# Sliding-window attention in a two-layer trunk: masked differences of values, one PSUM bank for both kv heads, scalar columns, queries by SyncE

## The chip, the cores and the metric

One Trainium2 chip, one core. The metric is the device time of one execution in microseconds. The kernel before takes 1153.45 us (median of 3 runs, 1150.15 to 1155.98).

## The reference, cut to what matters

A decoder trunk of two layers over 1024 tokens of 1024 features, in float32. Layer 0 is a pooling and short-convolution mixer with two large projections. Layer 1, which the change touches, is attention over a window of 128 tokens with 16 query heads of 64 columns, 2 key/value heads (8 query heads each) and a learned sink per head:

```
proj = y @ w_in + b_in                      # q, k, v and the gate z
q, k = partial_rotary(q), partial_rotary(k)
scores = (q . k) / 8, masked to 0 <= i + 128 - j < 128 over the previous and the own block
m   = max(max_j scores, sink)
p   = exp(scores - m);  p = p / (sum p + exp(sink - m))
out = p @ [v of the previous block; v of the own block]
h   = h + (out * silu(z)) @ w_out + b_out
return rms_norm(h, g)
```

Blocks are of 128 queries. A query i sees the keys j > i of the previous block and the keys j <= i of its own, so each pair of positions (i, j) in a 128x128 tile is taken from exactly one of the two blocks.

## The kernel before, in words

All products run on TensorE in float32r with operands split into a high and a low part (`split`: ScalarE casts the high part, VectorE subtracts for the low one), so a product is three matmuls. Layer 0's and layer 1's input projections use Strassen's scheme over pairs of output tiles (`Strassen.pair`; layer 1 has nine pairs, and their first partial products lie in `c1_dram` and are loaded back into `t3` tiles). `t3` is a pool of 128x512 tiles, 14 of them in layer 1. `W` is a pool of 9 raw tiles (weights, residual rows `h2`), `U` one of 16 split weight tiles that first hold the operands of Strassen's sums and later the output projection's weights.

The order of TensorE is the order of the program. The other engines' orders are a planner's, made from the program order and the planner's own costs; a tile whose buffers are all taken waits for a release.

Layer 1: the pairs for k and v, then four for q (stored transposed as high and low parts in `q_dram`), then four for the gate z (`z_pair`, L1122; silu on ScalarE in `gates`, stored in `z_dram`). Block 0 of the attention and the scores of block 1 are put between the products of the gate's pairs (`steps`). After them the loop over b from 1 to 8 (L1256) does, for each half js of the heads (two groups g of four heads each; one "step" below):

- `queries` (L1057): the queries of block b+1, loaded by GpSimd's queue straight into `qT` tiles, one step ahead;
- `probs` (L1143): the eight tiles of probabilities of block b are transposed on TensorE into a bank per group, split, and each part is masked twice by GpSimd (`affine_select`): strictly lower for the previous block's values, upper for the own;
- `scores` (L1065) of block b+1 in four pairs of heads: per head two matmuls against the keys of two blocks, then VectorE lays one block over the other by `copy_predicated` (so one 128x128 tile holds each score once), takes the maximum of a row, joins it with the sink (L1089), and ScalarE takes the exponential with its sum; `norm` scales by the reciprocal on GpSimd;
- `project` (L1192): the output projection of block b-1, eight groups of three matmuls; the pairs of scores come in at groups 1, 3, 4 and 6;
- `attend` (L1165): eight matmuls of 512 columns for the values of block b. The stationary operand holds a head's high and low values side by side, so a bank gets both in different partitions: ScalarE copies one half, VectorE adds it to the other, multiplies by the gate tile (loaded here by SyncE), and the result is split into `aH`, `aL`.

`summed` and `finish` add the residual, square, and apply the root (`rsqrt_mean` with n = 1, L130) and the final weights per block. PSUM has eight banks: during layer 1's pairs four called `b` and four `psB`; before the loop this pool is released and one with two `psA`, two `psD` and four `psB` made. The last four of the split weights needed first (`WO_FIRST`) are fetched among the gate's steps and split after the gates (L1254).

Of the kernel before, what the change touches and what calls it, by code (L numbers as in the profile page):

```python
# [18 lines left out]
P = 128  # L19
# [15 lines left out]
QT_BUFS = 6  # L35
# [39 lines left out]
def trunk(ctx, tc, x, xT, g1, pos, cols, w_in, w_pool, w_out, w_l1, b_kv, sinks, w_o, g_fin, out):  # L75
# [20 lines left out]
    def psA(name=None):  # L96
        if "l1" in pools:
            return psB()
        turn[0] += 1
        return pools["ps"].tile([P, HALF], F32, name=name or ("psA", "psD")[turn[0] % 2], bufs=2)  # L100
# [29 lines left out]
    def rsqrt_mean(pool, out_ap, sums, n, part=None):  # L130
# [13 lines left out]
        for it in range(3):  # L144
            if n == 1:
# [4 lines left out]
            stt(out=out_ap if it == 2 else y, in0=a, scalar=1.5, in1=y, op0=ALU.add, op1=ALU.mult)  # L150
# [714 lines left out]
    pools["ps"] = ps = tc.alloc_tile_pool(name="ps1", bufs=4, space=PSUM, reuse_waits="tile")  # L865
    pools["l1"] = True
# [37 lines left out]
    pools["t3n"] = 14  # L904
# [141 lines left out]
    qTs = {}  # L1046

    def load_q(b, js):
        if (b, js) not in qTs and b < NB:
            qTs[b, js] = [pe.tile([P, HALF], F32R, name="qT", bufs=QT_BUFS) for _ in range(2)]  # L1050
            for g, t in enumerate(qTs[b, js]):
                h = 8 * g + 4 * js
                nc.gpsimd.dma_start(out=t.rearrange("p (h c) -> p h c", c=P), in_=q_dram[
                    :, :, h:h + 4, b * P:(b + 1) * P].rearrange("a d h c -> (a d) h c"))


    def queries(b, js):  # L1057

        load_q(b, js)
        load_q(*((b, 1) if js == 0 else (b + 1, 0)))  # L1060
        return qTs.pop((b, js))
# [3 lines left out]
    def scores(b, js, qT):  # L1065
# [7 lines left out]
        def pair(g, i2):  # L1073
# [11 lines left out]
            else:  # L1085
# [36 lines left out]
    def z_pair(i, steps):  # L1122
# [3 lines left out]
        def most():  # L1126
            z_out.extend((2 * i + j, s_, o[j, s_]) for j, s_ in ((0, 0), (1, 1), (1, 0)))
            gates()

# [3 lines left out]

    vp = {}

    def values(b):

        t = pe.tile([P, 4, HD], F32R, name="vp", bufs=3)
        v = vtok[:, b, :].rearrange("p (g d) -> p g d", d=HD)
        split(t[:, 0::3, :], t[:, 1:3, :], v)  # L1140
        vp[b] = t

    def probs(b, js):  # L1143

        terms = []
        for g in range(2):
# [3 lines left out]
            curH, curL = t4(F32R), t4(F32R)  # L1150
            split(curH, curL, bank.rearrange("p (h c) -> p h c", c=P))
            if b:
                prvH, prvL = t4(F32R), t4(F32R)
                for a, t in ((prvH, curH), (prvL, curL)):
                    nc.gpsimd.affine_select(out=a, in_=t.bitcast(F32), pattern=[[0, 4], [-1, P]],
                                            compare_op=ALU.is_gt, fill=0.0, base=0,
                                            channel_multiplier=1)
                    nc.gpsimd.affine_select(out=t, in_=t.bitcast(F32), pattern=[[0, 4], [1, P]],
                                            compare_op=ALU.is_ge, fill=0.0, base=0,
                                            channel_multiplier=-1)  # L1160
                terms.append((vp[b - 1], g, prvH, prvL))
            terms.append((vp[b], g, curH, curL))
        return terms

    def attend(b, js, terms):  # L1165
        dst = []
        for g in range(2):
            bank = psA("psA")
            ops = [(v[:, 2 * g:2 * g + 2, :].rearrange("p a d -> p (a d)"), p)
                   for v, gg, h, lo in terms if gg == g for p in (h, lo)]  # L1170
            for i, (v, p) in enumerate(ops):
                mm(bank, lhsT=v, rhs=p, start=(i == 0), stop=(i == len(ops) - 1))  # L1172
            dst.append(bank.rearrange("p (j c) -> p j c", c=P))

        low, at, zt = t4(), t4(), t4()
        nc.sync.dma_start(out=zt, in_=z_dram[4 * js:4 * js + 4, :, b * P:(b + 1) * P].rearrange(
            "m p c -> p m c"))
        for g in range(2):
            own, other = slice(g * HD, (g + 1) * HD), slice((1 - g) * HD, (2 - g) * HD)
# [54 lines left out]
    for js in range(2):  # L1234
# [8 lines left out]
        z_pair(2 + js, steps)  # L1243
# [3 lines left out]
    ps.release()  # L1247
    pools["ps"] = ctx.enter_context(tc.tile_pool(name="ps2", bufs=4, space=PSUM,
                                                 reuse_waits="tile"))
    del pools["l1"]  # L1250
    end = ctx.enter_context(tc.tile_pool(name="end", bufs=1, side="right", reuse_waits="tile"))
    gfin = end.tile([P, D], F32, name="gfin")
    nc.sync.dma_start(out=gfin, in_=g_fin.to_broadcast([P, D]))
    for n, k2 in WO_FIRST:  # L1254
        load_wo(n, k2)
    for b in range(1, NB + 1):  # L1256
# [16 lines left out]
        for js in range(2):  # L1273
            steps = []
            if js == 0:
                h2 = W([P, D])
                sb, bb = divmod(b - 1, 4)
                nc.sync.dma_start(
                    out=h2.rearrange("p (f c) -> p f c", c=32),
                    in_=h1_dram[sb, :, bb * P:(bb + 1) * P, :].rearrange("f p c -> p f c"))  # L1280
# [73 lines left out]
```

## Time and profile before

| | |
|---|---|
| median of the runs | 1153.45 us |
| the profiled execution's own time | 1149.99 us |
| its span, first to last instruction | 1148.3 us |
| TensorE busy (matmuls) | 1064.3 us, 93% |
| VectorE busy | 853.7 us, 74% |
| ScalarE busy | 502.2 us, 44% |
| GpSimd busy | 184.2 us, 16% |
| mean granted TensorE clock | 0.974 |

Shares are means over stages with different limits. Up to some 720 us the kernel is layer 0 and its output projection, up to some 860 us layer 1's k, v and q; the gates run to some 935 us, the loop over blocks to the end. PE is TensorE's matmuls, PEld its weight loads, DVE VectorE, ACT ScalarE, POOL GpSimd, SP SyncE, which only issues DMAs. A matmul's duration runs into that of the next; the distance of two starts is what one costs.

### The profile page before, as it was taken

The page shows a single profiled execution, that of the slowest core. Times are in us where ns is not written, and L with a number is a line of the kernel's source. Part 1 is how long each engine was busy: PE and PEld are TensorE (multiplying, and loading weights), DVE is VectorE, ACT ScalarE, POOL GpSimd, SP SyncE. Part 2 cuts the span into 40 slices and gives each one's busy share as a digit, 9 for nine tenths or more (in the row PEclk, how much of TensorE's full clock was granted, in tenths as well). Part 3 has the DMA queues.
Part 4 walks back from the last instruction along what each step waited for, and adds up shares of the span by engine and source line. Part 5 has one row for each costly group of instructions (what it writes and reads, how often), then busy time and mean ns, then how long its engine had stood idle before and what let it go on. Part 6 is the DMA issues. An engine that isn't in the chain of part 4 may idle for free. (4 is left out here: it accounts for less than half of the span.)

```text
span 1148.3 us, 13822 instructions
## 1 busy us (share of the span) xinstructions
PE 1064.3 (93%) x4720; PEld 853.6 (74%) x4720; DVE 853.7 (74%) x1495; ACT 502.2 (44%) x1000; POOL 184.2 (16%) x285
## 2 busy tenths in 40 slices
PE   3999999999999999999999999999999768788897
PEld 3777888888888888887888888778777656666666
DVE  4799979957786769766536843876896759899984
ACT  4752332423233322434436533543444875455553
POOL 0000000000000000000000000021211316777773
PEclk9999999999999999999999999999998899989998
DMA  5343331222113120226535442653579599333211
GB/s 205 117 171 104 130 115 56 74 83 69 60 65 110 37 92 37 83 74 247 202 139 203 168 150 74 202 193 110 173 252 273 164 221 174 73 74 74 56 56 46
DMA packets 108133, 143.68 MB, mean 125 GB/s; under 512 B 39584, under 2 KB 64288, under 8 KB 108064
## 3 DMA queue, kind: packets, MB, share of 16 engines
q1 hardware_dynamic: 82960, 117.64, 32.4%
q0 software_dynamic: 16896, 8.39, 4.7%
q10 hardware_dynamic: 8208, 16.78, 4.0%
q8 instruction: 37, 0.61, 0.2%
q14 instruction: 32, 0.26, 0.1%
HBM read 106.35 MB, written 36.44 MB: 124 GB/s over the span
## 5 line engine op out<-in xcount | busy, mean ns | idle before, releaser
L180 ACT CAST W<-W 128x512 fp32r<-128x512 f32 (+1 forms) x234 | 156.3, 678 | 290.7 <-DVE W L362 104.1
L181 DVE TENSOR_TENSOR W<-W 128x512 fp32r<-128x512 f32 (+1 forms) x234 | 177.6, 768 | 106.7 <-ACT W L180 65.9
L387 PE MATMUL b<-U,W 128*128 128x512 f32 x432 | 109.8, 407 | 5.2 <-DVE W L181 2.7
L387 PEld LDWEIGHTS b<-U,W 128*128 128x128 f32 x432 | 81.8, 194 | 23.5 <-DVE W L181 3.1
L387 PE MATMUL b<-B22h,W 128*128 128x512 f32 x264 | 88.4, 396 | 3.0 <-DVE t L441 3.0
L387 PE MATMUL b<-B11h,W 128*128 128x512 f32 x264 | 88.7, 401 | 2.1 <-ACT W L180 1.2
L387 PE MATMUL b<-B21h,W 128*128 128x512 f32 x264 | 87.5, 396 | 1.1 <-ACT W L399 1.1
L387 PE MATMUL b<-T2h,W 128*128 128x512 f32 x192 | 65.4, 402 | 2.4 <-ACT W L180 2.4
L1092 ACT ACTIVATE pt<-psB,smax 128x128 f32<-128x128 f32 x128 | 45.7, 365 | 48.2 <-DVE smax L1089 32.3
L387 PE MATMUL b<-T1h,W 128*128 128x512 f32 x192 | 64.4, 396 | 0.0
L387 PE MATMUL b<-T3h,W 128*128 128x512 f32 x192 | 64.2, 395 | 0.0
L387 PE MATMUL b<-T4h,W 128*128 128x512 f32 x192 | 63.2, 390 | 0.0
L387 PEld LDWEIGHTS b<-B11h,W 128*128 128x128 f32 x264 | 50.4, 191 | 15.0 <-ACT W L180 1.6
L387 PEld LDWEIGHTS b<-B22h,W 128*128 128x128 f32 x264 | 49.6, 188 | 15.6 <-ACT t L985 3.3
L387 PEld LDWEIGHTS b<-B21h,W 128*128 128x128 f32 x264 | 49.6, 188 | 13.7 <-ACT W L399 2.0
L1203 PE MATMUL psD<-U,aH 128*128 128x512 f32 (+1 forms) x128 | 52.1, 407 | 6.9 <-DVE U L181 6.9
L689 POOL MEMSET T<- 128x16 f32 x8 | 0.9, 112 | 356.8 <-DVE T L623 227.8
L1202 PE MATMUL psD<-U,aH 128*128 128x512 f32 (+1 forms) x128 | 53.6, 419 | 2.2 <-ACT U L180 2.2
L827 PE MATMUL psD<-U,W 128*128 128x512 f32 x128 | 51.3, 401 | 2.6 <-DVE U L181 2.6
L387 PE MATMUL b<-B11l,W 128*128 128x512 f32 x132 | 52.9, 401 | 0.8 <-DVE B11l L471 0.8
L387 PE MATMUL b<-B21l,W 128*128 128x512 f32 x132 | 52.1, 395 | 0.0
L387 PE MATMUL b<-B22l,W 128*128 128x512 f32 x132 | 52.0, 394 | 0.0
(280 smaller groups left out, 2598.1 us busy)
## 6 DMA issues: line engine op xcount, KB each, us to landing
W<-w_in SPq DMA_DIRECT2D x54, 512.0 KB, 3.3
W<-w_out SPq DMA_DIRECT2D x32, 512.0 KB, 3.3
W<-w_l SPq DMA_DIRECT2D x27, 512.0 KB, 3.7
qT<-q_dram POOLq DMA_DIRECT2D x32, 256.0 KB, 3.8
o_dram<-t SPq DMA_DIRECT2D x30, 256.0 KB, 2.0
t<-c_dram SPq DMA_DIRECT2D x28, 256.0 KB, 4.0
c_dram<-W ACTq DMA_DIRECT2D x18, 256.0 KB, 3.1
T<-xT SPq DMA_DIRECT2D x16, 256.0 KB, 4.1
```

The lines of the kernel that those rows point to most:

```text
L180: nc.scalar.copy(out=dst_h, in_=src)
L181: sub(out=dst_l, in0=src, in1=dst_h.bitcast(F32), op=ALU.subtract)
L387: mm(dst, lhsT=w[:, hw, k], rhs=x[hx][:, k], start=start and k + n == 0, stop=k == 3 and n == 2, skip_group_check=not start)
L689: nc.gpsimd.memset(cu[:, 0:16], 0.0)
L827: mm(dst, lhsT=w[k][0], rhs=oHL[f][1], start=False, stop=False)
L1092: act(out=res[g][:, 2 * i2 + i, :], in_=bv[:, i, P:256], func=AF.Exp, scale=0.125, bias=smax[:, at + i:at + i + 1], accum_out=den[:, at + ...
L1202: mm(o, lhsT=a[0][:, kk, :], rhs=woH[8 * n + k][:, c], start=(k == 0), stop=False)
L1203: mm(o, lhsT=a[0][:, kk, :], rhs=woL[8 * n + k][:, c], start=False, stop=False)
```

## The change

Let V0 be the previous block's values, V1 the own block's, P the tile of probabilities and M the upper mask. Before: out = (P without M) V0 + (P with M) V1. After: out = P V0 + (P with M)(V1 - V0). So only one masked copy of each part is made. The values, and the differences (one subtraction on GpSimd per block), are kept as high and low tiles of three slots of 64 columns, `[v of head 0, 0, v of head 1]`; taking two neighbouring slots as the stationary operand puts a head's result in its own 64 partitions and adds zero in the other's, so both heads' matmuls add up in one bank, with three matmuls per term (high x high, low x high, high x low) in place of two. ScalarE's copies and VectorE's adds are gone, and the product with the gate reads PSUM. Block 0 has one term (its own values).

The rest: the maximum is joined with the sink by two `tensor_scalar` with columns in place of one `scalar_tensor_tensor`, the roots' steps likewise; queries are loaded by SyncE into `t3` tiles (12 of them now) and copied into `qT` by ScalarE; the gate tile has its own two buffers and is loaded a step ahead; `h2` and the final weights are issued behind a gate tile; the first four weights are split among the last gate's steps; the PSUM pool of layer 1 stays for the loop.

```diff
@@ rsqrt_mean, n == 1
-                stt(out=a, in0=y, scalar=h, in1=y, op0=ALU.mult, op1=ALU.mult)
+                ts(out=a, in0=y, scalar1=y, scalar2=h, op0=ALU.mult, op1=ALU.mult)
+                ts(out=z, in0=a, scalar1=1.5, scalar2=y, op0=ALU.add, op1=ALU.mult)
...
-    pools["t3n"] = 14
+    pools["t3n"] = 12
...
     def load_q(b, js):
-        if (b, js) not in qTs and b < NB:
-            qTs[b, js] = [pe.tile([P, HALF], F32R, name="qT", bufs=QT_BUFS) for _ in range(2)]
-            for g, t in enumerate(qTs[b, js]):
+        if (b, js) not in qraw and b < NB:
+            qraw[b, js] = [t4(), t4()]
+            for g, raw in enumerate(qraw[b, js]):
                 h = 8 * g + 4 * js
-                nc.gpsimd.dma_start(out=t.rearrange("p (h c) -> p h c", c=P), in_=q_dram[
-                    :, :, h:h + 4, b * P:(b + 1) * P].rearrange("a d h c -> (a d) h c"))
+                nc.sync.dma_start(out=raw, in_=q_dram[:, :, h:h + 4, b * P:(b + 1) * P].rearrange(
+                    "a d h c -> (a d) h c"))
     def queries(b, js):
+        if (b, js) in early:
+            return early.pop((b, js))
         load_q(b, js)
+        res = []
+        for raw in qraw.pop((b, js)):
+            t = pe.tile([P, HALF], F32R, name="qT", bufs=4)
+            nc.scalar.copy(out=t, in_=raw.rearrange("p h c -> p (h c)"))
+            res.append(t)
         load_q(*((b, 1) if js == 0 else (b + 1, 0)))
-        return qTs.pop((b, js))
+        return res
@@ scores
-            stt(out=m, in0=m, scalar=-0.125, in1=nsink[:, 8 * js + at:8 * js + at + 2],
-                op0=ALU.mult, op1=ALU.min)
             for i in range(2):
+                h = 8 * js + at + i
+                ts(out=m[:, i:i + 1], in0=m[:, i:i + 1], scalar1=-0.125, scalar2=nsink[:, h:h + 1],
+                   op0=ALU.mult, op1=ALU.min)
@@ values, now for v and v - previous v
+    vals = [[[pe.tile([P, 3, HD], F32R, name=f"v{n}{i}{j}", bufs=1) for n in "hl"]
+             for j in range(3 - i)] for i in range(2)]
+    for pair_ in vals[0] + vals[1]:
+        for t in pair_:
+            ts(out=t[:, 1], in0=ident[:, 0:HD], scalar1=0.0, scalar2=None, op0=ALU.mult)
...
+                ptt(out=v, in0=vtok[:, b, :], in1=vtok[:, b - 1, :], op=ALU.subtract)
+            vp[b, i] = vals[i][b % (3 - i)]
+            h, lo = (t[:, 0::2, :] for t in vp[b, i])
+            split(h, lo, v.rearrange("p (g d) -> p g d", d=HD))
@@ probs
-                prvH, prvL = t4(F32R), t4(F32R)
-                for a, t in ((prvH, curH), (prvL, curL)):
-                    nc.gpsimd.affine_select(out=a, in_=t.bitcast(F32), pattern=[[0, 4], [-1, P]],
-                                            compare_op=ALU.is_gt, fill=0.0, base=0,
-                                            channel_multiplier=1)
-                    nc.gpsimd.affine_select(out=t, in_=t.bitcast(F32), pattern=[[0, 4], [1, P]],
+            terms.append((vp[max(b - 1, 0), 0], g, h, lo))
+                own = t4(F32R), t4(F32R)
+                for a, t in zip(own, (h, lo)):
+                    nc.gpsimd.affine_select(out=a, in_=t.bitcast(F32), pattern=[[0, 4], [1, P]],
                                             compare_op=ALU.is_ge, fill=0.0, base=0,
                                             channel_multiplier=-1)
+                terms.append((vp[b, 1], g, *own))
@@ attend
+        bank = psA("psA")
         for g in range(2):
-            bank = psA("psA")
-            ops = [(v[:, 2 * g:2 * g + 2, :].rearrange("p a d -> p (a d)"), p)
-                   for v, gg, h, lo in terms if gg == g for p in (h, lo)]
+            ops = [(v[n][:, g:g + 2].rearrange("p a d -> p (a d)"), p)
+                   for v, gg, h, lo in terms if gg == g
+                   for n, p in ((0, h), (1, h), (0, lo))]
...
-            nc.scalar.copy(out=low[own], in_=dst[g][other])
-            tt(out=at[own], in0=dst[g][own], in1=low[own], op=ALU.add)
-        tt(out=at, in0=at, in1=zt, op=ALU.mult)
+        tt(out=at, in0=bank.rearrange("p (j c) -> p j c", c=P), in1=zts.pop((b, js)), op=ALU.mult)
+        if b or js:
+            load_z(*((b, 1) if js == 0 else (b + 1, 0)))
@@ the last gates and the loop
-            for i, a_ in enumerate(WO_FIRST):
-                steps[min(2 + i // 2, 4)].append(lambda a_=a_: fetch_wo(*a_))
+            for at_, f, i in ((0, fetch_wo, 0), (1, fetch_wo, 1), (1, fetch_wo, 2),
+                              (2, fetch_wo, 3), (2, load_wo, 0), (3, load_wo, 1),
+                              (3, load_wo, 2), (4, load_wo, 3)):
+                steps[at_].append(lambda f=f, i=i: f(*WO_FIRST[i]))
+            steps[2].append(lambda: early.update({(2, 0): queries(2, 0)}))
...
-    for n, k2 in WO_FIRST:
-        load_wo(n, k2)
...
+                with tc.issue_after(z_loads[b % NB, b // NB].ins):
+                    nc.sync.dma_start(
+                        out=h2.rearrange("p (f c) -> p f c", c=32),
+                        in_=h1_dram[sb, :, bb * P:(bb + 1) * P, :].rearrange("f p c -> p f c"))
```

`load_z(b, js)` loads the gate tile of a step into one of two `zt` buffers; for block 0 it is called behind the stores of the gates.

## Rows read from the trace of the kernel before

**Rows 1.** The page's span in 40 slices, busy tenths; PEclk is the granted clock.

```profile
PE   3999999999999999999999999999999768788897
DVE  4799979957786769766536843876896759899984
PEclk9999999999999999999999999999998899989998
```

**Rows 2.** Windows: length, busy us and count of PE, PEld, DVE, ACT, POOL, PEclk, DMA.

```profile
300.00:400.00 100.00, 100.00 (x432) 80.69 (x431) 75.70 (x111) 32.24 (x54) 0.45 (x4) 1.00 0.20 72
870.00:880.00 10.00, 7.33 (x29) 5.84 (x28) 5.25 (x11) 1.51 (x3) 0.00 (x0) 0.67 0.92 326
1014.70:1070.20 55.50, 48.26 (x232) 37.60 (x231) 50.22 (x111) 29.23 (x100) 41.28 (x53) 0.94 0.32 77
```

**Rows 3.** Timeline of PE (start, us): transposes, scores, and starts of value matmuls.

```profile
955.52 1.33 PE L1172 MATMUL psA<-t,vp 128*128 128x512 f32 x5
...
1016.61 1.03 PE L1149 MATMUL psB<-ident,pt 128*128 128x128 f32 x8
...
1018.18 0.28 PE L1080 MATMUL psB<-kT,qT 128*128 128x256 f32 x1
...
1018.30 0.28 PE L1081 MATMUL psB<-kT,qT 128*128 128x256 f32 x1
...
1104.61 2.03 PE L1172 MATMUL psA<-t,vp 128*128 128x512 f32 x8
...
1127.73 2.02 PE L1172 MATMUL psA<-t,vp 128*128 128x512 f32 x8
```

**Rows 4.** Lines of 1015 to 1071 us: count, busy us, mean ns, idle before.

```profile
L1089 DVE SCALAR_TENSOR_TENSOR smax<-smax,nsink 128x2 f32<-128x2 f32 x17 | 14.3, 840 | 0.0
...
L1155 POOL TENSOR_SCALAR_AFFINE_SELECT t<-t 128x512 fp32r<-128x512 f32 x16 | 9.9, 628 | 0.0
...
L1053 POOL DMA_DIRECT2D qT<-q_dram x9 | 7.1, 787 | 0.0
...
L1181 DVE TENSOR_TENSOR t<-psA,t 64x512 f32<-64x512 f32 x8 | 5.5, 687 | 0.5 <-ACT t L1180 0.4
...
L1180 ACT COPY t<-psA 64x512 f32<-64x512 f32 x8 | 4.6, 581 | 0.2
...
L181 DVE TENSOR_TENSOR aL<-t,aH 128x512 fp32r<-128x512 f32 x4 | 4.6, 1151 | 0.0
...
L146 DVE SCALAR_TENSOR_TENSOR rs_a<-rs_y,rs_h 128x1 f32<-128x1 f32 x6 | 2.7, 447 | 0.1
```

**Rows 5.** Single lines from 930 us on: duration ns min/median/max, first and last start.

```profile
L1089 DVE SCALAR_TENSOR_TENSOR smax<-smax,nsink x49: 142/358/3301, 930.7 to 1108.2; 128x2 f32<-128x2 f32 x49
L146 DVE SCALAR_TENSOR_TENSOR rs_a<-rs_y,rs_h x24: 212/220/998, 977.5 to 1143.2; 128x1 f32<-128x1 f32 x24
L139 DVE TENSOR_SCALAR rs_v<-ss x8: 213/214/215, 975.2 to 1141.8; 128x1 f32<-128x1 f32 x8
```

**Rows 6.** Timeline of DVE and POOL around 1025.6 us.

```profile
1025.60 3.27 DVE L1089 SCALAR_TENSOR_TENSOR smax<-smax,nsink 128x2 f32<-128x2 f32 x1
...
1025.61 1.22 POOL L1158 TENSOR_SCALAR_AFFINE_SELECT t<-t 128x512 fp32r<-128x512 f32 x2
1026.79 0.77 POOL L1053 DMA_DIRECT2D qT<-q_dram  x1
1027.57 1.28 POOL L1269 TENSOR_TENSOR W<-W,gfin 128x512 f32<-128x512 f32 x1
```

**Rows 7.** Timelines of DVE and PE in the gates stage; idle before, and its releaser.

```profile
873.15 0.69 DVE L432 TENSOR_TENSOR t<-b,t 128x512 f32<-128x512 f32 x1 [8.33 <-DMA t<-c_dram]
...
919.23 0.63 PE L1149 MATMUL psB<-ident,pt 128*128 128x128 f32 x4 [2.43 <-DVE t L1181]
...
944.26 0.69 DVE L1182 TENSOR_TENSOR t<-t,t 128x512 f32<-128x512 f32 x1 [5.25 <-DMA t<-z_dram]
...
947.28 0.80 PE L1203 MATMUL psD<-U,aH 128*128 128x512 f32 x1 [6.14 <-DVE U L181]
```

More of the change, by code (lines that the diff above doesn't have):

```diff
@@ L97, in psA @@
         if "l1" in pools:
-            return psB()
+            return pools["ps"].tile([P, HALF], F32, name=pools["l1"], bufs=4)
         turn[0] += 1
@@ L144, in rsqrt_mean @@
         for it in range(3):
+            z = out_ap if it == 2 else y
             if n == 1:
-                stt(out=a, in0=y, scalar=h, in1=y, op0=ALU.mult, op1=ALU.mult)
+                ts(out=a, in0=y, scalar1=y, scalar2=h, op0=ALU.mult, op1=ALU.mult)
+                ts(out=z, in0=a, scalar1=1.5, scalar2=y, op0=ALU.add, op1=ALU.mult)
             else:
@@ L149, in rsqrt_mean @@
                 stt(out=a, in0=a, scalar=-0.5, in1=v, op0=ALU.mult, op1=ALU.mult)
-            stt(out=out_ap if it == 2 else y, in0=a, scalar=1.5, in1=y, op0=ALU.add, op1=ALU.mult)
+                stt(out=z, in0=a, scalar=1.5, in1=y, op0=ALU.add, op1=ALU.mult)
     def diag_r(rcol, s):
@@ L864, in trunk @@
     ps.release()
-    pools["ps"] = ps = tc.alloc_tile_pool(name="ps1", bufs=4, space=PSUM, reuse_waits="tile")
-    pools["l1"] = True
+    pools["ps"] = ctx.enter_context(tc.tile_pool(name="ps1", bufs=4, space=PSUM,
+                                                 reuse_waits="tile"))
+    pools["l1"] = "psB"
     y11, y12, y21, y22 = Y["11"], Y["12"], Y["21"], Y["22"]
@@ L1120, in gates, with z_pair @@
         z_out.clear()
-    def z_pair(i, steps):
+    def z_pair(i, steps, then=lambda: None):
         o = {n: t3() for n in ((0, 1), (1, 0), (1, 1))}
@@ L1128, in most @@
             gates()
+            then()
         steps[3].append(most)
@@ L1134, in trunk, with load_z @@
     vp = {}
-    def values(b):
[L1138 to L1141, printed above, removed]
+    vals = [[[pe.tile([P, 3, HD], F32R, name=f"v{n}{i}{j}", bufs=1) for n in "hl"]
[3 more added lines that the diff above has]
+            ts(out=t[:, 1], in0=ident[:, 0:HD], scalar1=0.0, scalar2=None, op0=ALU.mult)
+    def values(b):
+        for i in range(2 if b else 1):
+            v = vtok[:, b, :]
+            if i:
+                v = pe.tile([P, P], F32, name="vd", bufs=1)
+                ptt(out=v, in0=vtok[:, b, :], in1=vtok[:, b - 1, :], op=ALU.subtract)
+            vp[b, i] = vals[i][b % (3 - i)]
+            h, lo = (t[:, 0::2, :] for t in vp[b, i])
+            split(h, lo, v.rearrange("p (g d) -> p g d", d=HD))
+    zts, z_loads = {}, {}
+    def load_z(b, js):
+        if b < NB:
+            zts[b, js] = zt = pe.tile([P, 4, P], F32, name="zt", bufs=2)
+            z_loads[b, js] = nc.sync.dma_start(out=zt, in_=z_dram[4 * js:4 * js + 4, :, b * P:(b + 1) * P]
+                              .rearrange("m p c -> p m c"))
     def probs(b, js):
@@ L1171, in attend @@
             for i, (v, p) in enumerate(ops):
[L1172 to L1179, printed above, removed]
-            nc.scalar.copy(out=low[own], in_=dst[g][other])
-            tt(out=at[own], in0=dst[g][own], in1=low[own], op=ALU.add)
@@ L1182, in attend @@
-        tt(out=at, in0=at, in1=zt, op=ALU.mult)
+                mm(bank, lhsT=v, rhs=p, start=(g == i == 0), stop=(g == 1 and i == len(ops) - 1))
+        at = t4()
+        tt(out=at, in0=bank.rearrange("p (j c) -> p j c", c=P), in1=zts.pop((b, js)), op=ALU.mult)
+        if b or js:
+            load_z(*((b, 1) if js == 0 else (b + 1, 0)))
         aH = pe.tile([P, 4, P], F32R, name="aH", bufs=3)
@@ L1246, in trunk @@
     tp.release()
[L1247 to L1250, printed above, removed]
+    pools["l1"] = "b"
     end = ctx.enter_context(tc.tile_pool(name="end", bufs=1, side="right", reuse_waits="tile"))
     gfin = end.tile([P, D], F32, name="gfin")
-    nc.sync.dma_start(out=gfin, in_=g_fin.to_broadcast([P, D]))
-    for n, k2 in WO_FIRST:
-        load_wo(n, k2)
     for b in range(1, NB + 1):
```

17 lines of the change are left out of this document (6 added, 11 removed).

## The prediction

> **What bounds the kernel now.** I read first the page's slices: TensorE is at nine tenths until three quarters of the span, and from there on it has holes while VectorE is as full as it ever was, and the granted clock drops in places [rows 1]. So the change, which touches the stage from some 850 us on, works where TensorE is no longer the only limit. Then the windows: 432 matmuls of 512 columns fill 100 us with no gap, so one costs 0.231 us at the full clock. The attention blocks, of which the window from 1014.7 to 1070.2 us holds four steps (a step is one half js of one block), take 13.9 us a step, with VectorE busy 50.22 of 55.5 us and TensorE 48.26, part of that at half clock (mean 0.94) [rows 2].
>
> What TensorE needs in a step is less: 8 transposes (1.0 us), 16 score matmuls 0.12 us apart (1.9), 24 projection and 8 value matmuls at 0.231 (5.6 and 1.9) [rows 2, 3]: 10.4 us. So 3.5 us a step are waits and slow clock, and VectorE with 12.6 busy us a step is the engine that sets them. The lines by group say why it is so full: a scalar_tensor_tensor of 128x2 elements costs 840 ns in the mean, and the low part aL 1151 [rows 4]. The spread of the single instructions is the key: the same line takes 142 ns at best and 3301 at worst, and the root's line 212 to 998, while tensor_scalar on the same columns, with one tensor and a column or constants, takes 213 to 215 [rows 5]. The timeline shows where the 3.27 us come from: the instruction starts with GpSimd's two masks at 1025.60, and ends when GpSimd's whole run (masks, a DMA issue, the multiply by gfin) ends, at 1028.9 [rows 6]. VectorE instructions with two SBUF tensors sit out GpSimd's work; those with one don't. The Trainium skill (SBUF — State Buffer, Who interferes with whom) has the same: a VectorE instruction with two SBUF inputs contends for a shared port pair with a GpSimd instruction that reads SBUF, and the loser blocks for the whole instruction; rows 6 agree, with 3.27 us for some 0.15 us of work.
>
> **The change part by part**, for one step of blocks 1 to 7 unless said.
>
> *Maxima.* Out: 4 scalar_tensor_tensors, 4 x 0.84 = 3.4 us. In: 8 tensor_scalars with a column; nearest row 0.20 to 0.215 [rows 4, 5], so 1.6 to 1.7. Bounds: 0.14 each (the old line's best, 1.1) and 0.84 each if they wait as the old ones did (6.7). I take 0.2: this row has the same operands. VectorE -1.7.
>
> *Roots.* Once a block, 6 instructions become 6; the old three at 447 wait like the maxima [rows 4], the new at 0.21. About -0.3 a step. In the tail they are on the path, but GpSimd is idle there: nothing.
>
> *Both kv heads in one bank, with padded values.* Out: two ScalarE copies (0.581 each) and two VectorE adds (0.687 each) [rows 4], -1.4 on VectorE. The product with the gate then reads PSUM directly; its price I leave. In: 12 value matmuls for 8, +4 x 0.231 = 0.92 us of TensorE a step, 60 matmuls or 13.9 us in all (56 in blocks 1 to 7 and 4 in block 0). This is the one sure cost.
>
> *Masked differences.* Out: the four L1155 masks, 4 x 0.63 = 2.5 us of GpSimd; the four of L1158 stay. In: one 128x128 subtraction on GpSimd and one more small split per block, 0.3 us or so each (an estimate: a quarter of the columns of the 128x512 rows, whose 0.63 and 1.15 bound it from above, and nothing from below). *Queries by SyncE.* Out: two GpSimd issues of 0.787 [rows 4], 1.6 us. GpSimd falls from 10.3 busy us a step [rows 2] to about 6, so aL and its like wait less (towards the 0.687 of the add that reads PSUM, -0.5). In: two ScalarE copies 128x512, about the 0.6 of the two that left. ScalarE stays at its 7.3 a step. The new wait is a copy's for its load, at the head of ScalarE's queue with the exponentials behind it; the load is issued a step (12 us) ahead, and SyncE now holds queries, gates and h2 in one order, h2 tied behind the gates. I price it at nothing while a load lands in under a step; each us that it is later costs the step a us.
>
> VectorE sums to 12.6 - 1.7 - 0.3 - 1.4 - 0.5 = 8.7 us a step, ScalarE 7.3, GpSimd 6, TensorE 10.4 + 0.92 = 11.3. TensorE is next. What then keeps a step above 11.3 is order: banks, and the waits between splits, masks and matmuls. I take 12.0, with 11.3 as lower bound (full clock, no hole) and 13.55 + 0.92 = 14.5 as upper (the matmuls are added and nothing else helps); nearer to the lower, since no other engine has more than 8.7.
>
> *The sum over the blocks.* Value matmuls of block 1, js 0 start at 955.5, those of block 6, js 1 at 1104.6: 11 steps, 149.1 us, 13.55 each. After: 132, -17.1. The next two steps, to 1127.7, take 23.1 [rows 3] and have no scores: 11.3 - 1.9 = 9.4, with 0.4 for order 9.8 each, 19.6, -3.5. From there to the end only the four more value matmuls of the last step count: +0.9.
>
> *Last weights among the gates, gates loaded ahead.* Before block 1 VectorE waits 5.25 us for the gate tile; the low parts of the first weights stand behind it, and TensorE idles 6.14 us for one of them and comes back slow, with 0.80 us for that matmul [rows 7]. With the weights split earlier, TensorE can go on until the scores lack banks; the gate tile itself comes no sooner, since it needs the last silu and its store. -5, between 0 (the hole only changes its name) and -11 (it closes, with the cold clock). What is late next is the product with the gate.
>
> *Gates stage.* The 2.43 us in which the transposes of block 0 wait for the adds [rows 7] go, -2.4; 4 more matmuls in block 0, +0.9; ten zero fills of 128x64, +0.3. Two fewer t3 buffers, and queries take t3 tiles: at 873 VectorE stands 8.33 us for an operand from c_dram, TensorE starves, and its granted clock is 0.67 of 2.4 GHz in the mean of 870 to 880, part of it at 1.2 [rows 2, 7]. That load now shares SyncE and t3 with six query loads. +1.5, between 0 and three more pairs with such a hole, +25.
>
> Sum: -17.1 - 3.5 + 0.9 - 5 - 2.4 + 0.9 + 0.3 + 1.5 = -24.4. The profiled run took 1149.99 us (span 1148.3); that makes 1125.6. The median shown is 3.46 above that run, so the median after is **1129 us**, own range 1119 to 1139 (a step at 11.3 gives -7.7, at 12.8 +8.8).
>
> **Rivals.**
> - *VectorE stays in the way* (1140 us, chance 0.18): the column form waits on GpSimd like the old one, or its queue order keeps a bank from TensorE; a step is 13.0, +11. For it: GpSimd still works 6 us a step. Against: the narrow spread in rows 5. In this rival the change does not do what it says. The Trainium skill (same section) speaks for it: tensor_scalar can enter two-port modes and then contends; the 128x1 rows in rows 5 show no such wait, and by that rule the sum would be this rival's.
> - *Nothing gained in the steps* (1149 us, 0.08): the chain of waits, not VectorE's load, sets 13.55; only the end's -3.5 and some 3 at the transition stay, less the added matmuls. Against: GpSimd's runs, which the stalls follow to the instruction [rows 6], get shorter by half.
> - *TensorE at its floor* (1116 us, 0.11): 11.3 a step (-7.7), transition -9 (-4), no loss in the gates stage (-1.5).
> - *SyncE and t3 block: slower* (1164 us, 0.09): the query loads stand in SyncE's order ahead of c_dram and weights and wait for t3 slots and for q_dram; each of three pairs gets the hole of 8.33 (+25 for the 1.5 taken), and late queries hold ScalarE a us in each of 11 steps (+11). For it: rows 7. Against: in most stretches the transfers fill a third of the engines (share 0.32 [rows 2]). It makes the kernel slower once these losses pass 30 us, i.e. all three holes and over half a us a step.
>
> **How the numbers follow.** Forecast 0.54. A measurement here tells 0.5% (5.8 us, below 1147.7 or above 1159.2) from no change. Faster: 0.54 + 0.18 + 0.11 + 0.02 of the second rival = 0.85; same: 0.06; slower: 0.09. The range 1112 to 1150 leaves out the slower rival and the far side of the floor, some 0.15.
>
> **What would show it.** Right: the maxima at about 0.2 us with no spread, GpSimd near 6 us a step, VectorE below 9, steps of 12 us with TensorE over nine tenths and the clock at 1.0, no weight split behind the gate tile at 940. Wrong: tensor_scalar of 128x1 at 1 us and more; scores waiting for VectorE as now; ScalarE standing before the copy of qT for a DMA; holes of 8 us at c_dram in more than one pair.

## The result, and the profile after

The changed kernel takes 1114.85 us (median of 4 runs, 1112.84 to 1115.1) and the kernel before, beside it, 1153.82 (4 runs, 1150.15 to 1155.98): a ratio of 0.966, 95% interval 0.963 to 0.969, or 39 us less. The forecast was 1129 us with an own range of 1119 to 1139; the time lies 14 us below it, outside the own range, inside the range of 1112 to 1150 and next to the rival "TensorE at its floor" (1116). The profiled execution took 1114.73 us, span 1112.9, against 1149.99 and 1148.3 before; so the spans, by which all that follows is told, show 35.4 of the 39 us.

The slices of the page, 40 equal parts of the span [rows 1]:

```profile
PE   3999999999999999999999999999989988999997
DVE  4699979967697578955744784397688777888874
PEclk9999999999999999999999999999989999999999
```

The sevens and eights of TensorE in the last quarter have become nines, but for three eights (807 to 835 and 890 to 946 us), and VectorE has fallen below it. The windows (length, then busy us and count of PE, PEld, DVE, ACT, POOL; PEclk; DMA share and GB/s), the second of four steps, as before [rows 2]:

```profile
870.00:880.00 10.00, 10.00 (x52) 8.35 (x51) 3.05 (x7) 4.11 (x7) 0.46 (x1) 1.00 1.08 364
982.70:1028.00 45.30, 45.04 (x241) 37.68 (x241) 38.71 (x122) 29.70 (x105) 25.35 (x30) 1.00 0.54 116
```

Four steps take 45.3 us for 55.5. Per step TensorE is busy 11.3 us of 11.3, VectorE 9.7 (12.6 before), ScalarE 7.4, GpSimd 6.3 (10.3), and the granted clock is 1.00. Starts of value matmuls on TensorE's timeline (start, us, engine line op out<-in) [rows 3]:

```profile
947.25 0.40 PE L1200 MATMUL b<-t,vh 128*128 128x512 f32 x1
...
1073.17 0.39 PE L1200 MATMUL b<-t,vh 128*128 128x512 f32 x1
...
1091.39 0.40 PE L1200 MATMUL b<-t,vh 128*128 128x512 f32 x1
```

From these starts the span divides into five parts. A step is called (block, js); the first two columns end at the value matmuls of (0,1) and (1,0), the 11 steps go from (1,0) to (6,1), the last two from (6,1) to (7,1). The second column, to (1,0), is called the transition below. All runs are in the table, since they are read by it:

| us | to (0,1) | to (1,0) | 11 steps | last two | rest | span |
|---|---|---|---|---|---|---|
| before | 932.3 | 23.2 | 149.1 | 23.1 | 20.6 | 1148.3 |
| after | 930.1 | 17.2 | 125.9 | 18.2 | 21.5 | 1112.9 |
| e1_no_columns | 929.7 | 17.5 | 136.1 | 18.2 | 21.6 | 1123.1 |
| e2_fewer_matmuls | 931.0 | 17.8 | 118.9 | 16.4 | 20.6 | 1104.7 |
| e3_columns_alone | 931.7 | 20.3 | 130.4 | 21.8 | 21.7 | 1125.9 |
| e4_masks_twice | 929.8 | 17.4 | 126.2 | 18.2 | 21.6 | 1113.2 |
| e5_weights_late | 931.7 | 16.3 | 127.1 | 18.2 | 21.5 | 1114.8 |
| e6_gpsimd_queries | 932.8 | 13.6 | 125.9 | 18.2 | 21.9 | 1112.3 |
| e7_old_values | 935.6 | 15.1 | 135.7 | 20.4 | 21.5 | 1128.3 |
| e8_last_gate_later | 931.8 | 17.4 | 126.1 | 18.2 | 21.6 | 1115.0 |
| e9_gates_late | 931.1 | 26.3 | 123.6 | 18.2 | 21.9 | 1121.1 |
| e10_gates_weights_late | 929.4 | 25.4 | 127.3 | 18.2 | 22.0 | 1122.3 |
| e11_weights_before_gfin | 930.9 | 13.6 | 122.5 | 18.2 | 21.8 | 1107.0 |
| e12_order_alone | 930.7 | 19.0 | 124.2 | 18.2 | 21.6 | 1113.6 |

Of the 35.4 us between the spans, 23.2 come from the 11 steps (13.55 to 11.45 each), 6.1 from the transition to block 1, 4.9 from the last two steps and 2.2 from the gates stage; the rest is 0.9 longer.

The lines by group of 985 to 1043 us (count, busy us, mean ns, idle before) [rows 4]:

```profile
L1187 POOL TENSOR_SCALAR_AFFINE_SELECT t<-t 128x512 fp32r<-128x512 f32 x20 | 13.7, 690 | 4.8 <-ACT t L181 2.3 <-DVE t L182 1.2 <-DVE smax L1100 0.9
L1100 DVE TENSOR_SCALAR smax<-smax,nsink 128x1 f32<-128x1 f32 x40 | 6.6, 205 | 0.3
L1067 ACT CAST qT<-t 128x512 fp32r<-128x512 f32 x10 | 6.2, 623 | 0.0
L182 DVE TENSOR_TENSOR aL<-t,aH 128x512 fp32r<-128x512 f32 x5 | 4.8, 952 | 1.4 <-ACT aH L181 1.4
L1110 DVE TENSOR_TENSOR es<-den,es 128x8 f32<-128x8 f32 x6 | 4.2, 697 | 3.6 <-ACT es L1109 3.6
L1202 DVE TENSOR_TENSOR t<-b,zt 128x512 f32<-128x512 f32 x6 | 4.1, 682 | 0.3
L182 DVE TENSOR_TENSOR vl<-vtok,vh 128x128 fp32r<-128x128 f32 x3 | 3.2, 1080 | 0.0
```

And single lines from 930 us on, duration in ns as min/median/max [rows 5]:

```profile
L1100 DVE TENSOR_SCALAR smax<-smax,nsink x98: 193/203/215, 931.3 to 1073.1; 128x1 f32<-128x1 f32 x98
L146 DVE TENSOR_SCALAR rs_a<-rs_y,rs_h x24: 254/272/275, 966.8 to 1108.0; 128x1 f32<-128x1 f32 x24
```

Where the maxima took 142 to 3301 ns, none of the 98 new ones leaves 193 to 215. The roots' first line is dearer than its median was (272 for 220), but the 998 is gone. The product L1202, whose price had been left open, takes 0.68 us. What still has two tensors in SBUF still waits, and some of it only now: aL takes 952 ns in the mean (0.70 us in the run e7_old_values), the sum of the denominators es 697 where it took 164 before, and the low part of the values 1080 where it took 279.

The hole of 8.33 us and the wait of 2.43 [rows 7] are gone, but there are others, two of them ahead of the gates (TensorE's timeline, idle before and its releaser in brackets):

```profile
824.84 4.59 PE L388 MATMUL b<-U,W 128*128 128x512 f32 x12 [1.88 <-ACT t L987]
...
831.93 4.61 PE L388 MATMUL b<-U,W 128*128 128x512 f32 x12 [2.21 <-DVE t L433]
...
903.96 1.09 PE L1180 MATMUL psB<-ident,pt 128*128 128x128 f32 x4 [3.04 <-POOL pt L1113]
```

The two groups of 12 take 4.6 us for the 3.0 that such a group takes elsewhere: the granted clock is 0.72 in the mean of 824 to 830 and of 831 to 837, part of it at 1.2 of 2.4 GHz. The wait before the transposes of 904 is not new: in the kernel before TensorE stands 3.54 us ahead of them.

### The profile page after: what moved, and what is told of

Same layout as the page of the kernel before. It is cut to its first block, busy times and chain, and to the rows that moved or that the text cites. A ratio compares the mean times of both kernels' runs of the same rounds, so it can differ in the third digit from the quotient of the medians.

```text
span 1112.9 us, 13964 instructions
## 1 busy us (share of the span) xinstructions
PE 1060.9 (95%) x4780; PEld 860.5 (77%) x4780; DVE 816.7 (73%) x1544; ACT 502.6 (45%) x1007; POOL 124.1 (11%) x204
## 5 line engine op out<-in xcount | busy, mean ns | idle before, releaser
L828 PE MATMUL psD<-U,W 128*128 128x512 f32 x128 | 51.3, 401 | 2.6 <-DVE U L182 2.6
L1225 PE MATMUL b<-U,aH 128*128 128x512 f32 (+1 forms) x128 | 49.8, 389 | 1.6 <-DVE U L182 1.6
L829 PE MATMUL psD<-U,W 128*128 128x512 f32 x128 | 51.1, 400 | 0.0
L827 PE MATMUL psD<-U,W 128*128 128x512 f32 x128 | 51.1, 399 | 0.0
```

The source lines that it names most:

```text
L827: mm(dst, lhsT=w[k][0], rhs=oHL[f][0], start=(f == 0), stop=False)
L828: mm(dst, lhsT=w[k][0], rhs=oHL[f][1], start=False, stop=False)
L829: mm(dst, lhsT=w[k][1], rhs=oHL[f][0], start=False, stop=(f == 15))
L1225: mm(o, lhsT=a[0][:, kk, :], rhs=woL[8 * n + k][:, c], start=False, stop=False)
```

## The experiments

Two theories stood at the start. One: in the steps VectorE was held by instructions that wait on GpSimd's runs, the columns take out the worst of them, and TensorE is now at its floor. The rival: GpSimd itself, with its masks and its issues, was what everything waited for, and its lighter load made the gain. Then the transition had to be given to one of the parts.

**The columns.** The first run undoes them in the kernel after, the third puts them alone into the kernel before.

```diff
-                ts(out=m[:, i:i + 1], in0=m[:, i:i + 1], scalar1=-0.125, scalar2=nsink[:, h:h + 1],
-                   op0=ALU.mult, op1=ALU.min)
+            stt(out=m, in0=m, scalar=-0.125, in1=nsink[:, 8 * js + at:8 * js + at + 2],
+                op0=ALU.mult, op1=ALU.min)
...
-                ts(out=a, in0=y, scalar1=y, scalar2=h, op0=ALU.mult, op1=ALU.mult)
+                stt(out=a, in0=y, scalar=h, in1=y, op0=ALU.mult, op1=ALU.mult)
```

> The changed kernel with the maxima and roots put back to scalar_tensor_tensor. Theory (TensorE is the limit now, VectorE has room): the four old maxima of a step wait for GpSimd again, but GpSimd has 6.3 us a step for 10.3, so some 0.5 us each; VectorE goes from 9.8 to about 10.5 us a step, below TensorE's 11.3. Steps of 11.5 to 12, 1115 to 1121 us. Rival (the column form is what freed the steps): the maxima stall for 1 to 3 us as before, the score banks come late, steps of 13, about 1132 us.

Measured: 1124.75 us (1122.56 to 1125.76), ratio 0.976 (0.974 to 0.978); some 10 us more than after, between the two expectations. The lines by group of 985.2 to 1035.2 us:

```profile
L1087 PE MATMUL psB<-kT,qT 128*128 128x256 f32 x32 | 8.8, 297 | 3.7 <-DVE smax L1096 3.7
...
L1096 DVE SCALAR_TENSOR_TENSOR smax<-smax,nsink 128x2 f32<-128x2 f32 x16 | 4.5, 280 | 0.3
L145 DVE SCALAR_TENSOR_TENSOR rs_a<-rs_y,rs_h 128x1 f32<-128x1 f32 x6 | 4.3, 718 | 0.1
...
L149 DVE SCALAR_TENSOR_TENSOR rs_y<-rs_a,rs_y 128x1 f32<-128x1 f32 x4 | 2.2, 554 | 0.1
```

With GpSimd at 6 us a step the old maxima cost only 280 ns each and not 840 [rows 4]; it is the roots, 718 and 554, that fall among GpSimd's runs. They come once a block, and so the steps alternate: 12.5 to 14.8, mostly 13.0, from js 1 to the next block's js 0, and 11.07 within a block from block 2 on, where no root stands. The runs that the roots fall among are GpSimd's multiplies by the reciprocals and by gfin (987.4 to 990.7 us), not its masks.

> The kernel before, with only the maxima and roots in the column form. Theory (VectorE's load and its waits on GpSimd set the step): VectorE falls by 2 us a step, steps of 13.55 to about 11.9, 1135 us. Rival (GpSimd's masks, or the chain from split to mask to matmul, set it): aL and the other two-tensor instructions take over the waiting; under 6 us gained, 1148 us or more.

Measured: 1124.83 us (1122.93 to 1127.62), ratio 0.976 (0.974 to 0.978). The step came as theory had it (11.86, 18.7 us over the 11), but the kernel became 27 us faster (22 by the span of the profiled execution) and not 17: the transition and the last two steps gave another 4. The window of four steps:

```profile
988.90:1036.50 47.60, 43.34 (x226) 34.16 (x225) 43.70 (x131) 30.37 (x106) 41.34 (x55) 1.00 0.40 95
```

GpSimd is as full as before (10.3 a step), and TensorE is busy 10.8 of 11.9. So the rival in its strict form falls. But the two halves don't add: the columns alone take 27 us, everything without the columns takes 27, and both together 39. Each takes VectorE's instructions out of GpSimd's way, the one by their form, the other by less of GpSimd, and what one has taken the other can't take again. That it is GpSimd's lighter load by which the other parts do this is not shown: no run fills GpSimd while the old maxima stand.

**GpSimd's load alone.** In the kernel after, each mask is made twice.

```diff
-                for a, t in zip(own, (h, lo)):
+                for a, t in list(zip(own, (h, lo))) * 2:
```

> The changed kernel with each of its masks made twice into the same tile: GpSimd gets 2.5 us a step more, 8.8, and nothing else changes. Theory (VectorE's column form does not wait for GpSimd, and it has room): under 4 us more, at most 1119 us. Rival (the halved masks are what freed the steps, by the waits of VectorE's two-tensor instructions and of the value matmuls): steps of 12.5 and more, 1127 us or more.

Measured: 1115.52 us (1114.86 to 1116.52), ratio 0.968. GpSimd rises from 6.3 to 9.0 us a step and nothing moves; the maxima stay at 198 to 215 ns:

```profile
983.00:1028.20 45.20, 44.96 (x241) 37.65 (x240) 39.35 (x121) 29.70 (x104) 35.86 (x48) 1.00 0.53 117
```

With the columns in place, four masks fewer a step are worth nothing that these runs can measure; es and aL, which still wait, take 681 and 955 ns here, as in the kernel after.

**TensorE's floor.** The kernel after without the 60 matmuls of the low part of the values.

```diff
-                   for n, p in ((0, h), (1, h), (0, lo))]
+                   for n, p in ((0, h), (0, lo))]
```

> The changed kernel without the 60 value matmuls low x high (the values' low part is left out of the result, all else stays). Theory (TensorE sets the step): each matmul left out gives back its 0.231 us, 13.9 us in all; steps of 10.5, about 1101 us. Rival (order, ScalarE or VectorE set the step at 11.45): 1110 us or more, with holes on TensorE in place of the matmuls.

Measured: 1106.36 us (1104.31 to 1106.97), ratio 0.960: 8.5 us of the 13.9 that these matmuls take on TensorE. Two windows, a step to the next block and one within it:

```profile
1003.40:1014.60 11.20, 10.34 (x57) 8.61 (x56) 10.44 (x33) 6.70 (x22) 6.67 (x8) 1.00 0.25 74
1014.60:1024.80 10.20, 10.20 (x57) 8.75 (x57) 9.04 (x28) 7.73 (x32) 6.14 (x7) 1.00 0.90 179
```

Within a block TensorE is full again at 10.2, so there it is the bound. In this step to the next block, as in four of five such, VectorE, busy 10.44 of 11.2, keeps TensorE waiting (0.86 us for a split at 1010.83): it is the second limit, and hardly an us behind.

**The old value part.** The kernel after with two banks, copies and adds, four masks a part and 8 matmuls.

```diff
-        bank = psA("psA")
         for g in range(2):
+            bank = psA("psA")
+            ops = [(v[:, 2 * g:2 * g + 2, :].rearrange("p a d -> p (a d)"), p)
+                   for v, gg, h, lo in terms if gg == g for p in (h, lo)]
...
+            nc.scalar.copy(out=low[own], in_=dst[g][other])
+            tt(out=at[own], in0=dst[g][own], in1=low[own], op=ALU.add)
```

> The kernel after, with the value part of the kernel before: two banks, the two copies and two adds, four masks a part, 8 value matmuls a step for 12. Theory (with the scalar columns VectorE has room, so that what the new value part takes off VectorE and puts on TensorE nearly cancels): TensorE's need falls by 0.92 us a step to 10.5, VectorE rises by 1.4 and more to 11.2 to 11.8, so steps of 11.5 to 12 and 1112 to 1121. Rival (the one bank is a main part of the gain): steps of 13 and more, 1130 to 1140.

Measured: 1129.75 us (1128.55 to 1130.68), ratio 0.981 (0.979 to 0.984), 15 us more than after. Both expectations missed, the rival by little: a step is 12.34 us although TensorE needs less. The lines by group of 991.85 to 1039.66 us, four steps:

```profile
L1089 PE MATMUL psB<-kT,qT 128*128 128x256 f32 x32 | 8.5, 289 | 2.3 <-DVE smax L1100 2.3
...
L1194 PE MATMUL b<-t,vp 128*128 128x512 f32 x32 | 9.6, 415 | 2.7 <-POOL t L1177 1.5 <-POOL t L1180 1.2
L1201 DVE TENSOR_TENSOR t<-b,t 64x512 f32<-64x512 f32 x8 | 5.5, 687 | 2.0 <-ACT t L1200 2.0
```

TensorE waits for masks ahead of the value matmuls and for VectorE ahead of the scores. In the old part every product of a step needs a mask; in the new one only those with the own block's difference do. So masks can be in the way here, though doubling them after the change cost nothing; that it depends on whether TensorE has other work until they are done is an argument and no run shows it. How much of the 15 us is masks and how much copies and adds was not taken apart.

**The transition.** First the weights split behind the gates again:

```diff
-                              (2, fetch_wo, 3), (2, load_wo, 0), (3, load_wo, 1),
-                              (3, load_wo, 2), (4, load_wo, 3)):
+                              (2, fetch_wo, 3)):
...
+    for n, k2 in WO_FIRST:
+        load_wo(n, k2)
```

> The kernel after, with its first four W_o weights split behind the gates again (as before the change); everything else as after. Theory (the weights among the gates give the transition its 6 us): the start of block 1's first value matmuls moves from 947.25 to 951..953, the stretch from (0,1) to (1,0) is 21 to 23 us again, and the time is 1119 to 1121. Rival (the transition gained because the steps around it hold less VectorE work, and the order of the splits is of no account): 1114 to 1116, the stretch stays at 17 to 18.

Measured: 1116.53 us (1115.52 to 1119.62), ratio 0.970; the transition stays short, 16.3. The weights' place did not make the gain. What it was after all is seen on the chain of the work that ended last (start, us, what), in the kernel before and then after:

```profile
934.36 6.46 DMA z_dram<-t
...
940.84 3.33 DMA t<-z_dram
...
944.26 0.70 DVE t L1182
```

```profile
936.16 2.41 DMA z_dram<-t
...
938.64 2.98 DMA zt<-z_dram
...
941.65 0.69 DVE t L1202
```

In both the gate tile's load leaves within 0.1 us of the landing of a gate's store, so before the change, too, nothing else in SyncE's queue held it, though the next expectation takes it so. But the store itself took 6.46 us to land before and takes 2.41 after, and VectorE's wait for the tile is 2.81 us for 5.25 [rows 7]. The windows of 930 to 940 us, before and then after:

```profile
930.00:940.00 10.00, 7.00 (x32) 5.52 (x31) 4.47 (x10) 9.09 (x18) 2.73 (x3) 0.91 0.96 308
```

```profile
930.00:940.00 10.00, 5.28 (x29) 3.97 (x27) 4.52 (x13) 9.50 (x20) 2.04 (x2) 1.00 0.37 134
```

The DMA engines were full (share 0.96), with gfin, weights and queries; after, h2 and gfin, and with them the later weights, leave only behind the gates' loads, and the share is 0.37.

So the gates' loads were undone next, with the weights early and with the weights late:

```diff
+        load_z(b, js)
         at = t4()
         tt(out=at, in0=bank.rearrange("p (j c) -> p j c", c=P), in1=zts.pop((b, js)), op=ALU.mult)
-        if b or js:
-            load_z(*((b, 1) if js == 0 else (b + 1, 0)))
...
-        z_pair(2 + js, steps, lambda js=js: load_z(0, js))
+        z_pair(2 + js, steps)
...
+    nc.sync.dma_start(out=gfin, in_=g_fin.to_broadcast([P, D]))
...
-                with tc.issue_after(z_loads[b % NB, b // NB].ins):
-                    nc.sync.dma_start(
+                nc.sync.dma_start(
```

> The kernel after with one part undone: each gate tile is loaded in the step that uses it, and h2 and gfin are no longer tied behind the gates' loads; the first weights stay among the gates. Theory (the transition gained because the gate's load no longer stands behind other work in SyncE's queue: it left 5.3 us after the last gate was stored in the kernel before, and 0.4 us after): the stretch from (0,1) to (1,0) is 20 to 23 us again, and the time is 1117 to 1121, steps unchanged. Rival (either order will do as long as the weights are split early): 16 to 18 and 1113 to 1116.

> The kernel after with both parts of the transition undone: the gates loaded in the step that uses them (as in the run with late gates) and the first weights split behind the gates (as in the run with late weights). Theory (the gates' loads alone made the gain): as with late gates alone, within 1 us. Rival (either part covers for the other): this one alone loses the 6 us, 1120 to 1123. Third (neither matters; the columns and the one bank shorten VectorE's queue there too): 1114 to 1117.

Measured: 1122.29 us (1120.49 to 1123.05), ratio 0.974 (0.973 to 0.976), and 1124.26 (1122.2 to 1125.19), ratio 0.976 (0.974 to 0.978). The transition takes 26.3 and 25.4 us. SyncE's timeline, the chain and VectorE's timeline of the first:

```profile
932.59 11.54 SPq L1297 DMA_DIRECT2D W<-h_dram  x2
...
944.23 5.89 DMA zt<-z_dram
...
950.14 0.69 DVE L1203 TENSOR_TENSOR t<-psB,zt 128x512 f32<-128x512 f32 x1 [8.81 <-DMA zt<-z_dram]
```

The DMA engines are full here too (share 1.02 from 930 to 940 us). The times of the gate tile in us; the second column is counted from the start of (0,1):

| | store to landing | product with the gate | from the product to (1,0) |
|---|---|---|---|
| before | 6.5 | 12.0 | 11.3 |
| after | 2.4 | 11.6 | 5.6 |
| e5_weights_late | 2.1 | 8.2 | 8.1 |
| e9_gates_late | 5.6 | 19.0 | 7.2 |
| e10_gates_weights_late | 9.0 | 15.8 | 9.5 |

So the short transition needs the gates' loads ahead and h2 and gfin tied behind them: with this undone the product comes 7.5 us later, and the kernel loses 7.4 us, more than the 6 won. Of the 7.5 the store's landing makes 3.2, the load's own landing 2.9 (5.89 for 2.98) and the place behind h2 in SyncE's queue 1.5; no run undoes the ties alone. The weights' place moves time from one side of the product to the other: with them among the gates ScalarE's casts of the weights stand ahead of the last silus and the product comes 3.4 us later (11.6 for 8.2), and what is behind it takes 2.5 us less. In all their place is worth at most 2 us either way, so neither rival holds.

> The kernel after, with the last gate's matmuls and silu (those of block 1's columns) moved from ahead of the loop to behind step (1,0). Theory (the 3.79 us in which TensorE waits for the exponentials at 940 come from ScalarE's order: the last silu and the two table loads stand ahead of them): the wait goes, 1111 to 1113. Rival (ScalarE's loads of its tables come once more in the loop, and the silu is in the way of exponentials there): 1115 to 1119.

Edit: the last `gates()` moves from ahead of the loop to behind step (1,0). Measured: 1116.55 us (1115.33 to 1118.57), ratio 0.970. The wait for the exponentials is 3.16 us instead of 3.79, the transition 17.4, a miss: the silu was not what stood in the way, or not alone.

**A faster version.** The queries by GpSimd again:

```diff
-            qraw[b, js] = [t4(), t4()]
+            qraw[b, js] = [pe.tile([P, HALF], F32R, name="qT", bufs=4) for _ in range(2)]
...
-                nc.sync.dma_start(out=raw, in_=q_dram[:, :, h:h + 4, b * P:(b + 1) * P].rearrange(
+                nc.gpsimd.dma_start(out=raw.rearrange("p (h c) -> p h c", c=P), in_=q_dram[:, :, h:h + 4, b * P:(b + 1) * P].rearrange(
...
-            nc.scalar.copy(out=t, in_=raw.rearrange("p h c -> p (h c)"))
...
-            steps[2].append(lambda: early.update({(2, 0): queries(2, 0)}))
```

> The kernel after, with the queries of each step loaded by GpSimd's queue straight into the tiles that the scores read, as before the change; the two ScalarE copies and the early load of the queries go. Theory (GpSimd's load no longer matters, as the doubled masks showed, and ScalarE's copies of 0.62 are hidden): 1113 to 1118, steps 11.4 to 11.6, ScalarE 1.2 busy us a step less, GpSimd 1.6 more. Rival (the queries' move is what freed VectorE): steps of 12.3, 1124.

Measured: 1113.23 us (1110.93 to 1115.66), ratio 0.967 (0.964 to 0.970), no difference from after. But inside it has moved: the transition takes 13.6 us, most steps 11.07, and the step from (1,0) to (1,1) 15.1. There TensorE and VectorE show:

```profile
953.85 3.98 DVE L182 TENSOR_TENSOR U<-W,U 128x1024 fp32r<-128x1024 f32 x2
...
955.90 0.50 PE L1222 MATMUL b<-U,aH 128*128 128x512 f32 x1 [2.26 <-DVE U L182]
```

The second half of W_o's weights is split late; SyncE had spent 4.28 us on gfin ahead of them. Hence the next edit, on top of this one and then on the kernel after alone:

```diff
+                after_ = z_loads[b % NB, b // NB]
+                if b == 1:
+                    with tc.issue_after(after_.ins):
+                        for k2 in (2, 3):
+                            for n in range(2):
+                                after_ = fetch_wo(n, k2)
+                h2 = W([P, D])
-                with tc.issue_after(z_loads[b % NB, b // NB].ins):
+                with tc.issue_after(after_.ins):
```

> A version that may beat the kernel after: the queries by GpSimd, as in the run with that name, and in SyncE's order the last four weights of W_o ahead of h2 and gfin, which are needed only at the end of a block. Theory (in that run SyncE spent 4.28 us on gfin, the weights landed from 949 on, and TensorE waited 0.76 and 2.26 us for their splits): the step from (1,0) to (1,1) shrinks from 15.1 to 12, 1109 to 1111. Rival (what is late is not the load but VectorE, whose two splits of the weights took 3.98 us beside GpSimd's masks): 1112 to 1114.

> The kernel after with only the order of SyncE changed: the last four weights of W_o ahead of h2 and gfin; the queries stay with SyncE and ScalarE's copies. Theory (the two parts of the faster version act at different places: the order gives the 0.76 and 0.81 us in which TensorE waits for splits of weights in the step from (1,0), the queries by GpSimd give the 3.8 us ahead of it and SyncE's room): 1112 to 1114, the step from (1,0) to (1,1) falls from 13.3 to 11.8, the stretch before it stays at 17. Rival (the order alone made the faster version): 1108 to 1110.

Measured: 1108.00 us (5 runs, 1107.45 to 1108.7), ratio 0.962 (0.961 to 0.964), against 1114.77 (1113.12 to 1117.67), ratio 0.968 (0.966 to 0.971), for the order alone. The first is the fastest of the kernels that compute the whole (the highest of its runs, 1108.7, lies below the lowest of the kernel after, 1112.84): its step from (1,0) takes 11.8 us, and from there TensorE has no gap left:

```profile
962.00:1070.00 108.00, 108.00 (x585) 92.64 (x584) 93.86 (x293) 61.56 (x231) 74.30 (x89) 1.00 0.67 118
```

The order alone shortens the same step (13.3 to 11.15) but lengthens the transition by nearly the same amount (17.2 to 19.0). The windows from the wait for the gates' product to the value matmuls of (1,0), of this run and then of the kernel after, with the same matmuls in both:

```profile
943.32:949.65 6.33, 6.33 (x20) 5.38 (x21) 5.42 (x9) 4.63 (x6) 2.31 (x3) 0.56 1.05 312
```

```profile
942.39:947.25 4.86, 4.86 (x21) 4.19 (x22) 4.75 (x14) 3.13 (x11) 2.31 (x3) 0.76 1.33 192
```

After two waits (3.79 us for the exponentials and then 1.02 for the gates' product, 0.27 in the kernel after) the matmuls of this run go at the lower level of 1.2 GHz for longer: TensorE is busy throughout in both, 6.33 us at a mean of 0.56 of 2.4 GHz against 4.86 at 0.76. That is 1.5 of the 1.9 us. So the two edits pay only together: the queries by GpSimd take ScalarE's copies and half of the wait before (2.04 us for 3.79), the order takes the wait behind.

## Why the prediction was right, and which terms were off

*The bound and its relief: right.* VectorE's instructions with two SBUF tensors were the ones that waited, the form with one tensor and a column does not, and with it TensorE is next. This is the mechanism of the rival "TensorE at its floor" too, which differed from the forecast by the sizes of the step, the transition and the gates stage alone; "Nothing gained in the steps" is refuted by 23.2 of 35.4 us. The rival "VectorE stays in the way" drew on a rule of the Trainium skill (SBUF — State Buffer, Who interferes with whom), that tensor_scalar can enter modes that take both ports and can then contend, where its operands meet conditions given elsewhere. For 128x1 operands no run here shows it: 98 instructions within 193 to 215 ns, and within 198 to 215 with the masks doubled.

*The step: 12.0 us forecast, 11.45 measured; the mis-sized terms.* TensorE's own need was put at 11.3 and is 11.07 us, the step of e11_weights_before_gfin in which it has no gap: the 1.0 us for eight transposes was a length that runs on past the last start, and from start to start they take 0.8. The 0.7 us for "order: banks, and the waits between splits, masks and matmuls" is 0.4, of which 0.2 is the first step alone (13.3 us, right behind the transition) and the rest the steps to a next block, at 11.5. Over 11 steps the two make 6.1 us of the 11 between the sum, -24.4, and the spans' difference, -35.4. VectorE was put at 8.7 and is 9.7: aL hardly waits less, and es and the low part of the values wait where they did not (697 for 164 ns, 1080 for 279). GpSimd and ScalarE came as forecast (6.3 for 6, 7.4 for 7.3).

*The last two steps: 9.8 forecast, 9.1 measured*, for the same reason; -4.9 for -3.5. The rest came as forecast, +0.9. The 3.46 us from the profiled run to the median were 0.12 in the kernel after, which is chance and makes the other 3 of the 14 us.

*The transition: -5 forecast, -6.1 measured; that the size came near is luck.* The prediction gave the -5 to the weights' new place and held that "the gate tile itself comes no sooner, since it needs the last silu and its store". Two things were left out. The weights' casts among the gates hold ScalarE, and the product with the gate comes 3.4 us later for them, so their new place alone is worth 2 us at most (e5_weights_late, e9_gates_late, e10_gates_weights_late). And the store's landing was taken as given, while it fell from 6.46 to 2.41 us with h2, gfin and the later weights behind the gates. The two nearly cancel in the time of the product, 11.6 us behind the start of (0,1) for 12.0; the gain shows behind it, where no weights wait for VectorE any more: 5.6 us for 11.3, and 8.1 with the weights late. Without the gates' part the transition is 9 us longer.

*The gates stage: +0.3 forecast, -2.2 measured.* (0,0) starts at 914.75 us and started at 914.80: all of the -2.2 lies between (0,0) and (0,1), where the 2.43 for the adds stood and is gone. The 8.33 us at c_dram are gone too, where +1.5 was set down for more of them, and TensorE is full from 870 to 880; but by the start of (0,0) nothing of this is left, with waits of 1.88 and 2.21 us earlier on and a slow clock behind each (820 to 840: 15.9 us busy at 0.83, and 17.4 at 1.00 before). Two runs say what did not close the hole: with the columns alone (e3_columns_alone) VectorE still waits 7.9 us for c_dram, and with the queries by GpSimd (e6_gpsimd_queries) TensorE stays full from 870 to 880. Which other part did was not tried. The starts of (0,0) differ by 2 us (914.42 to 916.47) among runs that are alike up to there, so a difference of that size in this stage is not explained here.

*SyncE and t3: not slower.* The query copies wait 0.2 us in all for q_dram over the attention stage. The price of the queries by SyncE is another, and only the faster version shows it: ScalarE's two copies and the order of SyncE keep the exponentials and the weights of block 1 late, and most steps to a next block take 11.5 us where they take 11.07 with the queries by GpSimd.

## What to carry to other kernels

Look at the spread of a line's single durations, not its mean: a line of 0.15 us of work with a maximum of 3.3 is waiting inside the instruction, and another form of the same operation can be free of it. When two sets of edits relieve the same engine, undo each alone before their gains are added: here the columns took 27 us, the rest without them 27, and both together 39. Loads that are needed a block later must not fill the DMA engines while a tile that is needed next is stored and loaded back: the time from the store's issue to its landing shows it, 6.46 us here with full engines and 2.41 without.

## What the runs showed that was not expected

- A wait of GpSimd's making falls on whichever two-tensor instruction stands beside its run: with GpSimd at 6.0 us a step the 128x2 maxima cost 280 ns in the mean and the 128x1 roots 718 (e1_no_columns), while at 10.3 us a step it was 840 and 447 [rows 4].
- With the columns in place GpSimd could be filled with masks from 6.3 to 9.0 us a step at no cost in time.
- A root's line with two column scalars takes 272 ns, the maxima's with one column and a constant 203.
